# A hybrid decoder block on one core: taking POOL's work in the mixer to DVE, ACT and PE, and preparing the first stage's chunks one ahead

## The chip, the cores and the metric

One core of a Trainium2 chip runs the whole block. Its engines are PE (TensorE, matrix products), DVE (VectorE, elementwise work), ACT (ScalarE, activations and copies), POOL (GpSimd) and SP (SyncE, which here issues nearly all DMAs). The metric is device microseconds (us) of one execution, as a median of runs; less is better. PE's clock is granted at one of two levels, 2.4 GHz (shown as 1.0) and 1.2 GHz (0.5).

## The reference, cut to what matters

256 tokens of width 1024 in float32. `c` is one conditioning vector; `ada` holds 48 columns of 128 numbers.

```python
ada = (silu(c) @ w_ada + b_ada)                 # w_ada is 1024 x 6144
sh1, sc1, g1, sh2, sc2, g2 = split(ada, 6)
h = rmsnorm(x, norm_pre_mix) * (1 + sc1) + sh1
proj = h @ w_in + b_in                          # xr, gr, q, k, v, gate_r, gate_a
xr = causal_depthwise_conv(xr, conv_w, conv_b)
y_rnn = rg_lru(xr, ...) * gelu(gr)              # sigmoid gates, exp decay, scan over tokens
y_att = swa_sink_attention(q, k, v, sinks)      # 16 heads, window 128
merged = sigmoid(gate_r) * (y_rnn @ w_o_rnn) + sigmoid(gate_a) * (y_att @ w_o_attn)
x = x + g1 * rmsnorm(merged @ w_out, norm_post_mix)
h = rmsnorm(x, norm_pre_ffn) * (1 + sc2) + sh2
x = x + g2 * rmsnorm(moe_ffn(h, ...), norm_post_ffn)   # top 4 of 32 experts
```

The experts' weights come in 384 loads of 1024 KB; the whole kernel reads 466.61 MB.

## The kernel before, in words

All weights pass through one ring of 18 slots of 8 KB a partition (`ring`). SP issues the loads in program order, and a load waits until the slot that it takes is released, so a load's time follows the work that frees slots.

**First stage (0 to about 73 us).** The loop over `k` (L210 to L240) makes the first 2048 columns of the projection. Chunk `k` needs two groups of columns of `ada` and one block of rows of the weights. `ada_dot` (L130) makes 128 numbers of `ada` on DVE: it multiplies a 128x1024 tile of transposed `w_ada` by silu(c), and its accumulator gives the sums. Then `am` (scale and shift), `hT` (the modulated input), and `split` (L161), which makes of a weight tile the pair `hi` (rounded, on ACT, L167) and `lo` (the rest, L170) in two halves of 128x1024. The first half's `lo` is DVE's, the second's POOL's. PE then makes three products, hi*hi, hi*lo and lo*hi, 48 matmuls of 256 columns a chunk (chunk 0 alone is 16 plain float32 matmuls, L229).

**Middle stretch (about 73 to 268 us): the mixer.** 22 steps (`step`, L509), each 48 matmuls of 128x128 by 256 columns (L260; step 5 at L179) in a PSUM bank of tag "p", of which there are three, taken in turn. Step `i` first splits the weights of step `i+1`, then empties the bank of step `i-1` (`late_work`), then multiplies. `PLAN` gives, by hand, the small tasks that run in the middle of step `i` and after it: "A" is a late tile of `w_ada` (two `ada_dot`s; 16 such tiles), s and c the convolution, m and R the gates, g and h the gelu, d, D, q and S the decay and scan, M, X, E, N, T and P attention (scores, maximum, exponentials, normalising, transposes, product with v). Each engine works its queue in program order. POOL has `lo` of each second half and the products of R (L343), g (L351), h (L356) and N (`att_norm`, L452).

**After it.** w_out, the second norm and the router (to about 325 us); then 32 experts, for which SP streams 12 MB each.

Of the kernel before, what the change touches and what calls it, by code (L numbers as in the profile page):

```python
# [50 lines left out]
def tile_hybrid_block(ctx: ExitStack, tc: tile.TileContext, x_in, c, vecs, rows, w_ada, w_g1, w_qk, w_v, w_gate,  # L51
# [108 lines left out]

    def split(w, pool=True, mid=lambda: None):  # L161
# [47 lines left out]

    for k in range(KC):  # L210
        if k:
# [5 lines left out]
        wt = rtile((2048,), "w")  # L217
        for h in range(2):
            nc.sync.dma_start(out=wt[:, h * D:(h + 1) * D], in_=w_g1[k, :, h * D:(h + 1) * D])
        nc.vector.scalar_tensor_tensor(am[:, 0, k:k + 1], ada[:, 8 + k:9 + k], scb[:, k:k + 1], v("n_pre_mix", k),  # L220
                                       op0=OP.add, op1=OP.mult)
        nc.vector.tensor_tensor(am[:, 1, k:k + 1], ada[:, k:k + 1], vec[:, o_ + k:o_ + k + 1], op=OP.add)
        if k == 1:
            lru_scales()
        hT[k] = t2((S,), name="hT")
        nc.vector.tensor_scalar(hT[k], xnT[:, k], am[:, 0, k:k + 1], am[:, 1, k:k + 1], op0=OP.mult, op1=OP.add)
        if k < PLAIN:
            for f in range(16):
                nc.tensor.matmul(g1(f), wt[:, f * P:(f + 1) * P], hT[k], start=k == 0 and f % 2 == 0, stop=False,  # L229
                                 skip_group_check=True)  # L230
        else:
            whl = split(wt, mid=lambda: split_h(k))
            for h in range(2):
                for i, (m, n) in enumerate(THREE):
                    for f in range(8):
                        nc.tensor.matmul(g1(8 * h + f), whl[h][m][:, f * P:(f + 1) * P], (hTh, hTl)[n][:, k], start=False,
                                         stop=k == KC - 1 and i == 2, skip_group_check=True)
# [219 lines left out]
    def att_turn(pr, blk, kbs):  # L457
        for kb in kbs:
            for half in range(2):
                b = bank("a", (4, P))  # L460
                for g in range(4):
                    t = att_tile(pr, half, blk, 0 if blk == 0 else g // 2 * 2)
                    gi = g if blk == 0 else g % 2
                    nc.tensor.transpose(b[:, g], t[:, gi, kb * P:(kb + 1) * P], ident)
                pT = pTs[kb, half] = t2((4, P))
                if half == 0:
                    nc.scalar.activation(pT, b, AF.Copy)
                else:
                    nc.vector.tensor_copy(pT, b)

# [106 lines left out]
    for i in range(22):  # L577
# [768 lines left out]
```

## Time and profile before

| | us |
|---|---|
| Median of 3 runs (1271.99 to 1273.15) | 1272.44 |
| The profiled execution's own time | 1274.03 |
| Its span in the profile | 1272.4 |
| Busy: PE, DVE, ACT, POOL | 1156.7, 525.9, 261.5, 135.8 |

The profile is of one execution. Times of rows count from the start of its span. A busy engine is not an engine at its peak: what matters is which engine the others wait for in each stretch.

### The profile page before, as it was taken

The numbers are of one execution on the slowest core, as the hardware profiler recorded it, in microseconds if no ns is written. First come the engines' busy times: TensorE is split into PE (matmuls) and PEld (weight loads), VectorE is DVE, ScalarE is ACT, GpSimd is POOL, SyncE is SP. The second block draws the span as 40 slices with busy tenths as digits, with TensorE's granted clock in tenths as the row PEclk, the third lists the DMA queues.
The fourth block names the chain that finished last, engine by engine and source line by source line (L and its number), as shares of the span: only waits on it lengthen the run. The fifth ranks groups of instructions, "written<-read, shape, count | busy, mean of one in ns | idle before, by whom it ended". The sixth has DMA issues, their size and how long they took to land. (4 is left out here: it accounts for less than half of the span.)

```text
span 1272.4 us, 15323 instructions
## 1 busy us (share of the span) xinstructions
PE 1156.7 (91%) x5883; PEld 556.6 (44%) x5883; DVE 525.9 (41%) x914; ACT 261.5 (21%) x482; POOL 135.8 (11%) x79
## 2 busy tenths in 40 slices
PE   7897978869899999999999999999979999998886
PEld 5796757767433333333343333333323333332322
DVE  6999988965242222223221232322222323222222
ACT  4364656324311001010000011100100111000002
POOL 2455545321010000000000000000000000000000
PEclk9998989889999999999989989999979999999998
DMA  9963436667979999999999999999999999999995
GB/s 364 392 247 135 181 116 265 265 230 289 419 302 400 421 420 421 421 422 421 421 422 419 423 386 421 422 421 420 421 420 421 421 421 421 421 421 422 421 421 222
DMA packets 68176, 468.72 MB, mean 368 GB/s; under 512 B 7616, under 2 KB 8000, under 8 KB 13696
## 3 DMA queue, kind: packets, MB, share of 16 engines
q1 hardware_dynamic: 67392, 466.67, 89.6%
q10 hardware_dynamic: 704, 1.01, 0.3%
q8 instruction: 47, 0.77, 0.2%
q14 instruction: 33, 0.27, 0.1%
HBM read 466.61 MB, written 1.05 MB: 368 GB/s over the span
## 5 line engine op out<-in xcount | busy, mean ns | idle before, releaser
L964 PE MATMUL bank_a<-w,xg 128*64 128x512 f32 x2048 | 471.7, 606 | 11.2 <-DVEq L1126 6.5
L964 PEld LDWEIGHTS bank_a<-w,xg 128*64 128x64 f32 x2048 | 139.9, 139 | 292.8 <-issue 262.9
L997 PE MATMUL bank_a<-w,aT 128*64 128x512 f32 x960 | 216.8, 600 | 9.2 <-ACT aT L991 7.4
L1045 DVE TENSOR_SCALAR G<-bank_p,slot 128x256 fp32r<-128x256 f32 x32 | 15.5, 484 | 409.2 <-PE bank_p L1040 409.2
L997 PEld LDWEIGHTS bank_a<-w,aT 128*64 128x64 f32 x960 | 66.0, 137 | 142.1 <-issue 115.4
L991 ACT ACTIVATE aT<-bank_p 128x512 f32<-128x512 f32 x31 | 18.5, 597 | 524.7 <-PE bank_p L987 524.7
L1018 DVE TENSOR_TENSOR ff<-ff,bank_p 128x512 f32<-128x512 f32 x124 | 79.7, 684 | 64.7 <-PE bank_p L1015 64.7
L170 POOL TENSOR_TENSOR lo<-w,hi 128x1024 fp32r<-128x1024 f32 x32 | 89.2, 2789 | 132.5 <-ACT hi L167 105.7
L1260 POOL TENSOR_TENSOR os<-os,x 128x512 f32<-128x512 f32 x1 | 1.3, 1261 | 869.7 <-DVE rs L665 869.7
L131 DVE SCALAR_TENSOR_TENSOR w<-w,cs 128x1024 f32<-128x1024 f32 x48 | 89.0, 1892 | 1.0 <-DMA w<-in_w_ada_dram 1.0
L1005 DVE SCALAR_TENSOR_TENSOR ys<-bank_a,gslot,ys 128x512 fp32r<-128x512 f32 x31 | 23.3, 750 | 146.8 <-ACT ys L1004 146.8
L167 ACT ACTIVATE hi<-w 128x1024 fp32r<-128x1024 f32 x66 | 66.0, 1050 | 11.6 <-DVE lo L170 6.8
L1015 PE MATMUL bank_p<-ys,G 64*128 64x512 f32 x248 | 49.7, 474 | 14.3 <-DVE ys L1005 13.5
L1004 ACT ACTIVATE ys<-bank_a,gslot 128x512 fp32r<-128x512 f32 x31 | 21.3, 688 | 167.7 <-PE bank_a L997 164.1
L170 DVE TENSOR_TENSOR lo<-w,hi 128x1024 fp32r<-128x1024 f32 x34 | 46.8, 1381 | 6.5 <-ACT hi L167 6.5
L778 PE MATMUL bank_p<-pm,hth 128*128 128x256 f32 x112 | 31.9, 317 | 13.5 <-DVE pm L760 13.5
L1015 PEld LDWEIGHTS bank_p<-ys,G 64*128 64x128 f32 x248 | 20.4, 198 | 48.2 <-issue 25.2
L960 PE MATMUL bank_a<-b1r,pick 128*128 128x512 f32 x124 | 37.7, 423 | 0.0
L778 PEld LDWEIGHTS bank_p<-pm,hth 128*128 128x128 f32 x112 | 21.6, 192 | 35.9 <-issue 18.3
L977 ACT ACTIVATE ys<-gl 128x512 f32<-128x512 f32 x33 | 20.8, 630 | 74.9 <-DVE gl L976 74.9
L960 PEld LDWEIGHTS bank_a<-b1r,pick 128*128 128x128 f32 x124 | 20.7, 188 | 29.4 <-issue 26.8
L976 DVE TENSOR_SCALAR gl<-bank_a 128x512 f32<-128x512 f32 x33 | 22.6, 686 | 23.0 <-PE bank_a L964 17.2
(337 smaller groups left out, 1258.9 us busy)
## 6 DMA issues: line engine op xcount, KB each, us to landing
w<-in_w_dram SPq DMA_DIRECT2D x383, 1024.0 KB, 19.8
w<-in_w_ada_dram SPq DMA_DIRECT2D x16, 1024.0 KB, 5.0
w<-in_w_ada_dram SPq DMA_DIRECT2D x16, 512.0 KB, 10.1
w<-in_w_g_dram SPq DMA_DIRECT2D x16, 512.0 KB, 10.2
w<-in_w_gate_dram SPq DMA_DIRECT2D x8, 1024.0 KB, 5.8
w<-in_w_qk_dram SPq DMA_DIRECT2D x5, 1024.0 KB, 8.3
w<-in_w_oa_dram SPq DMA_DIRECT2D x4, 1024.0 KB, 6.8
w<-in_w_or_dram SPq DMA_DIRECT2D x4, 1024.0 KB, 5.9
```

Of the source, the lines that this page charges most:

```text
L131: nc.vector.scalar_tensor_tensor(wt[:, n], wt[:, n], 1.0, sc_, op0=OP.mult, op1=OP.mult, accum_out=ada[:, j:j + 1])
L167: nc.scalar.activation(hi[:, c_], w[:, c_], AF.Copy)
L170: (nc.gpsimd if h and pool else nc.vector).tensor_tensor(lo[:, c_], w[:, c_], hi[:, c_], op=OP.subtract)
L778: nc.tensor.matmul(ps[:, n], z[:, t, f * P:(f + 1) * P], pms[:, t].rearrange("p a b -> p (a b)"), start=t == 0 and n == 0 if len(ts) == 1 ...
L960: nc.tensor.matmul(o, m.rearrange("p a b -> p (a b)"), z, start=False, stop=False)
L964: nc.tensor.matmul(o[q * CAP:(q + 1) * CAP], xk(k), w1t[k][:, c0:c0 + 512], start=k == 0, stop=k == KC - 1)
L976: nc.vector.tensor_scalar(gl, bb[0], LIMIT, None, op0=OP.min)
L997: nc.tensor.matmul(y[q * CAP:(q + 1) * CAP], aT[:, k % 4, k // 4 * CAP:(k // 4 + 1) * CAP], w2t[k // 2][:, k % 2, q * 512:(q + 1) * 512], ...
L1004: nc.scalar.activation(hi, y, AF.Copy, scale=G[1])
L1005: nc.vector.scalar_tensor_tensor(lo, y, G[1], hi, op0=OP.mult, op1=OP.subtract)
L1015: nc.tensor.matmul(b[q], G[0][qs, t * P:(t + 1) * P], ys[i][qs], start=i == 1, stop=i == 0)
L1018: nc.vector.tensor_tensor(d, d, b[q], op=OP.add)
```

## The change

The order in `PLAN` and `ISSUE` stays. `split` gives both halves of `lo` to DVE. The products of R, h and N go from POOL to DVE; the gelu's polynomial becomes a Square on ACT and one product on DVE; the decay's square goes to ACT; the second half's copies of transposed probabilities (T) go from DVE to ACT; the emptying of `gr` goes to ACT and half of that of `xr` to DVE. Six of the 16 late tiles of `w_ada` (positions 2, 4, 5, 7, 9 and 11 of their order) come in untransposed layout, and PE multiplies them: `ada_mm` (8 matmuls with a stationary of 32 equal columns, four groups of output partitions, then a copy on ACT), and at the next list of tasks `ada_sum` (2 matmuls with one column, then a copy on ACT). In the first stage, iteration `k` prepares chunk `k` and then issues the matmuls of chunk `k-1`; `hT` is made on ACT, and silu(c) is made once more in another layout (`scc`).

```diff
+ON_PE = (2, 4, 5, 7, 9, 11)
...
     nc.scalar.activation(warm, eps, AF.Sqrt)
+    scc = consts.tile([P, KC], F32, name="scc")
+    nc.scalar.activation(scc, v("c"), AF.Sigmoid)
+    nc.vector.tensor_tensor(scc, v("c"), scc, op=OP.mult)
+    one_each = consts.tile([P, 1], F32, name="one_each")
+    nc.vector.tensor_reduce(one_each, ident.rearrange("p (a b) -> p a b", a=4)[:, :, 0], axis=AX.X, op=OP.add)
...
+    def ada_mm(wt):
+
+        b = bank("p")
+        for k in range(KC):
+            q = k % 4
+            nc.tensor.matmul(b[32 * q:32 * q + 32, 0:2 * P], scc[:, k:k + 1].to_broadcast([P, 32]),
+                             wt[:, k * 2 * P:(k + 1) * 2 * P], start=k < 4, stop=k >= 4)
+        r = wt[:, 0:2 * P]
+        nc.scalar.activation(r, b[:, 0:2 * P], AF.Copy)
+        return b, r
+
+    def ada_sum(b, r, j):
+
+        for n in range(2):
+            nc.tensor.matmul(b[:, 2 * P + n:2 * P + n + 1], r[:, n * P:(n + 1) * P], one_each, start=True, stop=True)
+        nc.scalar.activation(ada[:, j:j + 2], b[:, 2 * P:2 * P + 2], AF.Copy)
...
-            (nc.gpsimd if h and pool else nc.vector).tensor_tensor(lo[:, c_], w[:, c_], hi[:, c_], op=OP.subtract)
+            nc.vector.tensor_tensor(lo[:, c_], w[:, c_], hi[:, c_], op=OP.subtract)
...
+    for k in range(KC + 1):
+        if 0 < k < KC:
             wada.append(rtile((2, D), "w"))
...
+            def make_h(k=k):
+                nc.scalar.activation(hT[k], xnT[:, k], AF.Identity, scale=am[:, 0, k:k + 1], bias=am[:, 1, k:k + 1])
+                nc.scalar.activation(hTh[:, k], hT[k], AF.Copy)
+
+            if k < PLAIN:
+                make_h()
+                whl[k] = wt
+            else:
+                whl[k] = split(wt, make_h)
+                low_h(k)
+        if k:
+            m_ = k - 1
+            w_ = whl.pop(m_)
+            if m_ < PLAIN:
...
+                low_h(m_)
+            else:
+                for m, n in THREE:
+                    for f in range(16):
+                        nc.tensor.matmul(g1(f), w_[f // 8][m][:, f % 8 * P:(f % 8 + 1) * P], (hTh, hTl)[n][:, m_],
+                                         start=False, stop=m_ == KC - 1 and m == 1, skip_group_check=True)
...
     def ada_run(j):
+        if j in on_pe:
+            w = late[j].rearrange("p a b -> p (a b)")
+            sums_due.append((*ada_mm(w), 2 * j))
+            return
...
-        nc.gpsimd.tensor_tensor(i_, xcs[u], i_, op=OP.mult)
+        nc.vector.tensor_tensor(i_, xcs[u], i_, op=OP.mult)
...
-        nc.vector.tensor_tensor(z, g, g, op=OP.mult)
-        nc.vector.tensor_scalar(z, z, 0.044715, 1.0, op0=OP.mult, op1=OP.add)
-        nc.gpsimd.tensor_tensor(z, z, g, op=OP.mult)
+        nc.scalar.activation(z, g, AF.Square, scale=math.sqrt(0.044715))
+        nc.vector.scalar_tensor_tensor(z, z, 1.0, g, op0=OP.add, op1=OP.mult)
...
-        nc.gpsimd.tensor_tensor(g, z, g, op=OP.mult)
+        nc.vector.tensor_tensor(g, z, g, op=OP.mult)
...
-        nc.vector.tensor_tensor(z, a_, a_, op=OP.mult)
+        nc.scalar.activation(z, a_, AF.Square)
...
-            nc.gpsimd.tensor_tensor(t, t, den[:, blk, gs[0]:gs[0] + len(gs), None].to_broadcast(list(t.shape)),
+            nc.vector.tensor_tensor(t, t, den[:, blk, gs[0]:gs[0] + len(gs), None].to_broadcast(list(t.shape)),
...
-                if half == 0:
-                    nc.scalar.activation(pT, b, AF.Copy)
-                else:
-                    nc.vector.tensor_copy(pT, b)
+                nc.scalar.activation(pT, b, AF.Copy)
...
+        if f % 2:
+            nc.vector.tensor_scalar(xr[:, f, 3:], b_, v("b_xr", f), None, op0=OP.add)
+        else:
+            nc.scalar.activation(xr[:, f, 3:], b_, AF.Identity, bias=v("b_xr", f))
...
     def run(tasks):
 
+        while sums_due:
+            ada_sum(*sums_due.pop())
...
-                nc.vector.tensor_scalar(gr[:, f], b_, v("b_gr", f), None, op0=OP.add)
+                nc.scalar.activation(gr[:, f], b_, AF.Identity, bias=v("b_gr", f))
...
+    by_feature = a["w_ada"].T.reshape(48, P, D)[ada_order].reshape(24, 2, P, D).transpose(0, 2, 1, 3)
+    by_chunk = a["w_ada"].reshape(KC, P, 48, P)[:, :, ada_order].reshape(KC, P, 24, 2 * P).transpose(2, 1, 0, 3)
```

## Rows read from the trace of the kernel before

**Rows 1.** Windows: stretch, us, busy us (PE, PEld, DVE, ACT, POOL), clock, DMA share, GB/s
```profile
0.00:72.60 72.60, 58.58 (x396) 51.49 (x397) 59.73 (x101) 31.82 (x48) 24.42 (x19) 1.00 0.98 378
72.60:268.00 195.40, 169.29 (x1257) 151.81 (x1257) 182.10 (x241) 106.49 (x207) 97.49 (x47) 0.92 0.50 190
...
400.00:1015.00 615.00, 584.40 (x2690) 214.70 (x2687) 162.97 (x301) 59.66 (x108) 0.00 (x0) 0.98 1.01 419
1015.00:1236.00 221.00, 203.75 (x933) 69.97 (x931) 58.92 (x109) 20.50 (x36) 0.00 (x0) 1.00 1.01 421
```

**Rows 2.** Chain that ended last: start us, us, what
```profile
1015.70 19.77 DMA w<-in_w_dram
...
1235.39 1.94 PE bank_a L964 x8
```

**Rows 3.** Waits of PE, 72.6 to 268 us: total, times, longest (of seven lines)
```profile
PE bank_a L476 <- DVE t L469: 8.4, 2, 5.1
PE bank_a L406 <- DVE att L425: 6.2, 2, 4.8
```

**Rows 4.** Timeline of DVE, 60 to 156 us: start us, us, instruction
```profile
60.72 3.42 DVE L131 SCALAR_TENSOR_TENSOR w<-w,cs 128x1024 f32<-128x1024 f32 x1
...
64.07 1.21 DVE L131 SCALAR_TENSOR_TENSOR w<-w,cs 128x1024 f32<-128x1024 f32 x1
...
152.99 2.95 DVE L323 SCALAR_TENSOR_TENSOR xc<-xr,vec,xc 128x256 f32<-128x256 f32 x6
```

**Rows 5.** Timeline of POOL from 60 us
```profile
60.23 2.82 POOL L170 TENSOR_TENSOR lo<-w,hi 128x1024 fp32r<-128x1024 f32 x1 [4.49 <-ACT hi L167]
```

**Rows 6.** Groups by line on DVE, 72 to 268 us
```profile
L131 DVE SCALAR_TENSOR_TENSOR w<-w,cs 128x1024 f32<-128x1024 f32 x32 | 58.9, 1884 | 0.0
L170 DVE TENSOR_TENSOR lo<-w,hi 128x1024 fp32r<-128x1024 f32 x23 | 33.5, 1458 | 0.3 <-ACT hi L167 0.3
L323 DVE SCALAR_TENSOR_TENSOR xc<-xr,vec,xc 128x256 f32<-128x256 f32 x24 | 21.6, 918 | 0.6
...
L469 DVE COPY t<-bank_a 128x512 f32<-128x512 f32 x6 | 4.1, 683 | 1.8 <-POOL rnn L343 1.8
```

**Rows 7.** Waits of PE, 0 to 130 us
```profile
PE bank_p L236 <- ACT hTh L185: 8.8, 7, 1.6
```

**Rows 8.** Timeline of PE from 95 us
```profile
95.81 1.94 PE L334 MATMUL bank_a<-xc,cs 64*64 64x256 f32 x16
97.69 1.22 PE L260 MATMUL bank_p<-hTh,hi 128*128 128x256 f32 x8
98.75 1.12 PE L260 MATMUL bank_p<-hTl,hi 128*128 128x256 f32 x8
```

**Rows 9.** Timeline of ACT, first 34 us
```profile
7.20 1.28 ACT L121 ACT_TABLE_LOAD   x1
8.49 0.20 ACT L121 ACTIVATE small<-small 128x1 f32<-128x1 f32 x1
...
14.58 1.55 ACT L147 ACTIVATE xnT<-bank_a 128x512 f32<-128x512 f32 x3
```

**Rows 10.** Timeline of PE, first 30 us
```profile
14.59 2.86 PE L229 MATMUL bank_p<-hT,w 128*128 128x256 f32 x12 [0.86 <-DVE hT L226]
```

**Rows 11.** DMA issues of the page: KB each, median us to landing
```profile
w<-in_w_g_dram SPq DMA_DIRECT2D x16, 512.0 KB, 10.2
```

**Rows 12.** Groups by line on POOL, 72.6 to 268 us
```profile
L170 POOL TENSOR_TENSOR lo<-w,hi 128x1024 fp32r<-128x1024 f32 x23 | 64.6, 2810 | 64.7 <-ACT hi L167 53.4 <-DVE w L131 7.6 <-issue 2.2
L452 POOL TENSOR_TENSOR att<-att,den 128x512 f32<-128x512 f32 x12 | 13.9, 1184 | 11.4 <-DVE den L449 11.4
```

**Rows 13.** Timeline of PE, 236 to 345 us
```profile
273.78 1.87 PE L709 MATMUL bank_p<-rw,ada 128*128 128x32 f32 x16
...
285.64 1.12 PE L599 MATMUL bank_p<-ident,ada 128*128 128x128 f32 x4 [9.52 <-DVE t L569]
```

**Rows 14.** Groups by line on ACT, 72 to 270 us
```profile
L443 ACT ACTIVATE att<-att,nm 128x128 f32<-128x128 f32 (+1 forms) x32 | 14.1, 444 | 0.0
```

More of the change, by code (lines that the diff above doesn't have):

```diff
@@ L41 @@
                ("b_xr", 8), ("b_gr", 8), ("b_q", 8), ("b_k", 2), ("b_ga_r", 8), ("b_ga_a", 8),
-               ("cw0", 8), ("cw1", 8), ("cw2", 8), ("cw3", 8), ("cb", 8), ("rba", 8), ("rbx", 8), ("lam", 8)):
+               ("cw0", 8), ("cw1", 8), ("cw2", 8), ("cw3", 8), ("cb", 8), ("rba", 8), ("rbx", 8), ("lam", 8), ("c", 8)):
     VEC[_n] = (_o, _w)
@@ L158, in tile_hybrid_block, with split @@
     nc.vector.memset(xr[:, :, 0:3], 0.0)
-    def split(w, pool=True, mid=lambda: None):
+    def split(w, mid=lambda: None):
         hi, lo = [ring.tile([P, 2 * D], F32R, name=n_, tag="w") for n_ in ("hi", "lo")]
@@ L182, in tile_hybrid_block @@
     hTl = ring.tile([P, KC, S], F32R, name="hTl", tag="w")
-    def split_h(k):
-        nc.scalar.activation(hTh[:, k], hT[k], AF.Copy)
-        nc.vector.tensor_tensor(hTl[:, k], hT[k], hTh[:, k], op=OP.subtract)
     def lru_scales():
@@ L208, in g1, with low_h @@
         return g1b[f // 2][:, (f % 2) * S:(f % 2 + 1) * S]
-    for k in range(KC):
-        if k:
+    def low_h(k):
+        nc.vector.tensor_tensor(hTl[:, k], hT[k], hTh[:, k], op=OP.subtract)
+    whl = {}
+    for k in range(KC + 1):
+        if 0 < k < KC:
             wada.append(rtile((2, D), "w"))
@@ L216, in tile_hybrid_block @@
             ada_dot(wada[k], 1, 8 + k)
[L217 to L230, printed above, removed]
-        else:
-            whl = split(wt, mid=lambda: split_h(k))
-            for h in range(2):
[L234 to L237, printed above, removed]
@@ L238, in tile_hybrid_block @@
-        if 4 <= k < 4 + PLAIN:
-            split_h(k - 4)
+        if k < KC:
+            wt = rtile((2048,), "w")
+            for h in range(2):
+                nc.sync.dma_start(out=wt[:, h * D:(h + 1) * D], in_=w_g1[k, :, h * D:(h + 1) * D])
+            nc.vector.scalar_tensor_tensor(am[:, 0, k:k + 1], ada[:, 8 + k:9 + k], scb[:, k:k + 1], v("n_pre_mix", k),
+                                           op0=OP.add, op1=OP.mult)
+            nc.vector.tensor_tensor(am[:, 1, k:k + 1], ada[:, k:k + 1], vec[:, o_ + k:o_ + k + 1], op=OP.add)
+            if k == 1:
+                lru_scales()
+            hT[k] = t2((S,), name="hT")
+            def make_h(k=k):
[7 more added lines that the diff above has]
+                low_h(k)
@@ new lines, in tile_hybrid_block @@
+        if k:
[3 more added lines that the diff above has]
+                for f in range(16):
+                    nc.tensor.matmul(g1(f), w_[:, f * P:(f + 1) * P], hT[m_], start=m_ == 0 and f % 2 == 0, stop=False,
+                                     skip_group_check=True)
+                low_h(m_)
+            else:
+                for m, n in THREE:
+                    for f in range(16):
+                        nc.tensor.matmul(g1(f), w_[f // 8][m][:, f % 8 * P:(f % 8 + 1) * P], (hTh, hTl)[n][:, m_],
+                                         start=False, stop=m_ == KC - 1 and m == 1, skip_group_check=True)
@@ L297, in tile_hybrid_block @@
     late = {}
+    sums_due = []
     def ada_run(j):
+        if j in on_pe:
+            w = late[j].rearrange("p a b -> p (a b)")
+            sums_due.append((*ada_mm(w), 2 * j))
+            return
         for n in range(2):
@@ L465, in att_turn @@
                 pT = pTs[kb, half] = t2((4, P))
-                if half == 0:
-                    nc.scalar.activation(pT, b, AF.Copy)
-                else:
-                    nc.vector.tensor_copy(pT, b)
+                nc.scalar.activation(pT, b, AF.Copy)
     def att_apply(pr, blk):
@@ L489, in tile_hybrid_block @@
     order = [(E // 2 + i) % E for i in range(E)]
-    w_in_, whl, w1_first = {}, {}, []
+    w_in_, w1_first = {}, []
     rest = [*range(8, 12), *range(16, 20), *range(12, 16), *range(20, 24)]
     order_a = list(rest)
+    on_pe = [rest[i] for i in ON_PE]
     assert "".join(ISSUE.values()).count("w") == NW and "".join(ISSUE.values()).count("a") == len(rest)
@@ L512, in step @@
         if i + 1 < NW:
-            whl[i + 1] = split(w_in_[i + 1], i < 24)
+            whl[i + 1] = split(w_in_[i + 1])
         for f in late_work:
@@ L534, in tile_hybrid_block @@
         b_ = g1b[f // 2][:, (f % 2) * S:(f % 2 + 1) * S]
-        nc.scalar.activation(xr[:, f, 3:], b_, AF.Identity, bias=v("b_xr", f))
+        if f % 2:
+            nc.vector.tensor_scalar(xr[:, f, 3:], b_, v("b_xr", f), None, op0=OP.add)
+        else:
+            nc.scalar.activation(xr[:, f, 3:], b_, AF.Identity, bias=v("b_xr", f))
     bks = {}
     def run(tasks):
+        while sums_due:
+            ada_sum(*sums_due.pop())
         for task in tasks.split():
@@ L584, in tile_hybrid_block @@
                 b_ = g1b[4 + f // 2][:, (f % 2) * S:(f % 2 + 1) * S]
-                nc.vector.tensor_scalar(gr[:, f], b_, v("b_gr", f), None, op0=OP.add)
+                nc.scalar.activation(gr[:, f], b_, AF.Identity, bias=v("b_gr", f))
         run(after)
+    assert not sums_due
     nc.vector.tensor_tensor(ada[:, 16:48], ada[:, 16:48], vec[:, o_ + 16:o_ + 48], op=OP.add)
@@ L1308 @@
     ada_order = [j for k in range(8) for j in (k, 8 + k)] + list(range(16, 48))
-    w_ada = a["w_ada"].T.reshape(48, P, D)[ada_order].reshape(24, 2, P, D).transpose(0, 2, 1, 3)
+    by_feature = a["w_ada"].T.reshape(48, P, D)[ada_order].reshape(24, 2, P, D).transpose(0, 2, 1, 3)
+    by_chunk = a["w_ada"].reshape(KC, P, 48, P)[:, :, ada_order].reshape(KC, P, 24, 2 * P).transpose(2, 1, 0, 3)
+    late = [*range(8, 12), *range(16, 20), *range(12, 16), *range(20, 24)]
+    w_ada = by_feature.copy()
+    for i in ON_PE:
+        w_ada[late[i]] = by_chunk[late[i]].reshape(P, 2, D)
     vecs = np.concatenate([cols(z) for z in (
@@ L1312 @@
         bi[0], bi[1], bi[2], bi[3], bi[5], bi[6], a["conv_w"][0], a["conv_w"][1], a["conv_w"][2], a["conv_w"][3],
-        a["conv_b"], a["rg_b_a"], a["rg_b_x"], a["rg_lambda"])], axis=1)
+        a["conv_b"], a["rg_b_a"], a["rg_b_x"], a["rg_lambda"], a["c"])], axis=1)
     rows = np.concatenate([bi[4], a["attn_sinks"], a["router_b"]])[None]
```

## The prediction, made before the change was run

> **What bounds the kernel now.** I read the windows first, cut where the program's stages meet [rows 1]. From 400 us on the DMA engines are full (share 1.01, 419 to 421 GB/s) in both stretches, and the chain that ended last runs over the experts' loads from 1015.70 to 1235.39 us, with only PE's short end behind [rows 2]. So the end is the start of that full stream plus a fixed number of bytes: a microsecond taken from the mixer, where the DMA share is 0.50, moves the end by a microsecond, since the loads follow the slots that the mixer frees. A microsecond on any engine after 400 us is worth nothing. In the middle stretch (195.4 us) DVE is busy 182.1 us, PE 169.3 at a granted clock of 0.92, ACT 106.5, POOL 97.5. DVE is the engine without air; PE's idle 26 us there are nearly all waits for DVE, led by 8.4 us for copies of attention (L469) and 6.2 for its maxima (L425) [rows 3].
>
> Why DVE is so full is seen in two neighbouring rows: of two equal `ada_dot`s, the one that meets POOL's `lo` (60.23 us, 2.82 long) takes 3.42 us and ends about when POOL ends, the next one, alone, 1.21 [rows 4, 5]. In the middle stretch the mean is 1.884 for the dots, 1.458 for `lo`, 0.918 for the convolution's 256 columns [rows 6]. So much of DVE's 182 us is waiting on POOL, inside its instructions.
>
> **First stage.** PE waits 8.8 us in all for the chunks after the first [rows 7]; the period is set by DVE: the long dot 3.42, the clear one 1.21, and a chain of small steps through ACT. Afterwards DVE has two dots, two `lo` of the second kind (4 times 1.21, 4.9) and, by my estimate, 0.6 of small ones, 5.5 us a chunk, against PE's 48 matmuls at 0.12 (eight in 0.96, from 98.75 minus 97.69 with the start-up of 0.1 left out), 5.8 [rows 8]. PE is then the bound and, with a chunk ready ahead, waits no more: minus 8.8 us. Against it stands the start. The new Sigmoid for `scc` comes behind the warm Sqrt, and the Sqrt of the norm behind it needs its table again: two loads of 1.28 [rows 9] and 0.2, so 2.7 us later. And `hT` of chunk 0 is now made by ACT, behind the four copies that end at 16.1 in the row, where DVE had it for the first matmul at 14.59 [rows 9, 10]: 16.1 plus 0.4 (under the 0.52 of one of those three copies, which have twice the columns) plus 2.7 is 19.2, so PE starts 4.6 us later. PE's idle time before it grows too; half clock for part of chunk 0 I put at 0.9 (between 0 and 2). Net minus 3.3 (between minus 1 and minus 6).
>
> The loads cover this. SP's order is unchanged, and of the 18 slots three are held throughout, so at four slots a chunk the weights of chunk 7 wait until PE has used `hi` of chunk 3. By the times above that is near 42 us; with 10.2 us to landing [rows 11] they are there at 52, and DVE, 5.5 a chunk after a start near 25, comes to them at 53. Each us that they are later is a us lost.
>
> The row shows the load at 1.28 us with the activation 0.01 behind it. The Trainium skill (ScalarE: Activation LUTs, What ACT_TABLE_LOAD costs) gives 2.66 us a switch with the drain, which would make the start 2.8 us worse; the trace does not show that drain.
>
> **Middle stretch, DVE.** With POOL silent I price by the clear row, 1.21 to 1.22:
> - dots: 32 become 20, 58.9 to 24.4
> - `lo`: 23 become 46, 33.5 to 56.1
> - convolution: 24 at 0.49 (six together, clear of POOL, took 2.95 [rows 4]) instead of 0.918, 21.6 to 11.8
> - from POOL: 12 products of N and 12 of R, g and h, all 128x512, at 0.68 (the size of L469 [rows 6]; POOL took 1.184 [rows 12]): plus 16.3
> - gone to ACT or merged: six copies, eight emptyings of 256 columns, the squares and scalings, some 22 passes of that size: minus 14
> - the rest, 182.1 less those three groups, 68.1, holds contention too: I estimate that 9 of it go, between 0 and that.
>
> Sum 24.4 + 56.1 + 11.8 + 16.3 - 14 + 68.1 - 9 = 154 us (163 if the rest keeps its contention), down from 182.
>
> **Middle stretch, PE.** The 22 steps are 1056 matmuls at 0.12, 127 us; 22 times 5.76. The small products (L334 in 1.9 a time [rows 8], scores, transposes, v) add some 28, counted at full clock: 155. That agrees with 169.3 busy less what the half clock costs (0.08 of 195.4, at most 15.6).
>
> New on PE: `ada_mm`, eight float32 matmuls of 256 columns. No row shows four groups side by side. Lower end: the pairs of L964 run two groups of 512 columns in 0.97 (eight records, 1.94, are two pairs [rows 2]), so four groups of 256 might take 0.5 and eight matmuls 1.0. Upper end: one after another as in L229 (12 records, 2.86, are six matmuls, 0.45 each [rows 10]): 3.6. I take 1.0, since L964 too splits output partitions into groups. `ada_sum` is two small ones at 0.23 (16 records of L709 in 1.87 are eight [rows 13]), 0.5. Six tiles: 9 us (up to 25).
>
> Changing the tile shape costs something: behind L334 (64*64) the first eight matmuls take 1.22 where the next take 1.12, so 0.1 [rows 8]; 12 switches, 1.2 us, lie inside my rounding. The Trainium skill (TensorEngine Tiling (Array Packing), Key Properties) says that changing the tiling mode drains the engine; the 0.1 is what the trace shows of that.
>
> So PE's floor is 155 + 9 = 164, DVE 154 to 163, ACT about 120 (106.5 and some 14 for the passes moved to it). PE becomes the bound, with little air on DVE.
>
> **What is still waited for.** The order in `PLAN` is unchanged, and ACT now stands where DVE stood. After step 5 come two tiles on PE and E; there are three banks "p", and step 6 takes the one that step 5 filled, so PE waits until DVE has emptied it. DVE's queue there holds D, whose square waits on ACT behind E's eight exponentials (14.1 / 4 = 3.5 us and about 1.5 of accumulator reads [rows 14]), then two `lo`, 2.4. From the last scores to there PE has v's 5.8, two tiles at 1.0 and the next scores (1.2), 9 us; the other two have the maxima (3), E (5), the square and its product (1.2), `lo` (2.4) and the emptying (0.7), one behind the other, 12 to 13: about 4 us. The waits for copies of transposed probabilities move from DVE to ACT, which has E's 5 us in front in steps 7 to 10: three places at some 2, so 6 of the 8.4. Steps 13 to 16 (three scans) and 19 (two tiles): 3. Half clock behind such gaps: 3. Together 16 (between 5 and 25). Stretch: 164 + 16 = 180 against 195.4, minus 15.4.
>
> The slots of the six tiles come free at `ada_sum`, half a step after PE has read them; no weight of the mixer was waited for by ACT's `hi` in this stretch, and the DMA share of 0.50 leaves room, so I price that at nothing (its cover gone, a step's split would wait for one landing).
>
> **Tail to 325 us.** `lo` moves to DVE in front of merge_r (plus 1.2), whose products lose POOL's contention (my estimate: minus 1.6). The 9.5 us that PE waits there [rows 13] hang on the b1 loads that ACT waits for; they stay. Minus 0.4.
>
> Sum: 3.3 + 15.4 + 0.4 = 19.1 off 1274.03 is 1254.9; the median of before lies 1.6 under its profiled execution, so 1253.3, say 1253.
>
> **Rivals.**
> - *PE floor.* ACT keeps up and the waits shrink under 9 us, the start costs less. For it: ACT has 75 us of air in the stretch. Against it: three engines at 120 to 164 of 175 in fixed order. Gain 26 to 35: 1238 to 1246.
> - *ACT or DVE takes over.* The queues stand behind one another in the order given, and waits come to 25 or more, or `ada_mm` runs one after another (6 times 2.6, plus 15.6). Gain 4 to 13: 1260 to 1269.
> - *The end doesn't move.* If the expert loads started when they do now, by bandwidth alone, the time would stay 1272. Against it: share 0.50 in the mixer, and loads that wait for slots.
> - *Slower: DVE's long rows are its own.* If a dot stays 1.884 and `lo` 1.458 with POOL idle, DVE's stretch gets 182.1 - 22.6 + 33.5 + 16.3 - 14 = 195.3, and with the 13 us that it idled 208: plus 13; first-stage chunks get plus 0.9 each (another `lo`, less `hT`), with 4.6 at the start plus 11. 1296. The point is a mean of about 1.37 per 128x1024 pass: 66 of them, 92 of others and 13 idle make 195. The two neighbouring rows speak against it.
>
> **How the numbers follow.** Forecast 0.62, 1246 to 1260; floor 0.12; ACT, DVE or `ada_mm` 0.16; end unmoved 0.04; slower 0.06. The predicted time is the first's, 1253. The range 1240 to 1264 takes in most of the floor and half of the third case, whose bounds (waits 5 to 25, `ada_mm` 1.0 to 3.6, start 1 to 6) are those above. Within 0.2% (2.5 us) a measurement of this kernel can't tell from no change: faster 0.90, same 0.04, slower 0.06.
>
> **What would show it.** Dots and `lo` at 1.22 throughout; the first matmul near 19 us, chunks every 5.8 to 5.9, and the first stage ending near 69; PE with the longest busy time in a middle stretch of some 180; one `ada_mm` within 1 us; a wait near 4 us ahead of step 6; the expert stream full some 19 us earlier, and the same 421 GB/s after it. I am wrong if a new table load or copy on ACT stands ahead of PE in most steps, if DVE rows stay long, or if the stream's start does not move.

## The result, and the profile after

The changed kernel takes 1257.2 us (median of 4 runs, 1255.7 to 1258.1) against 1272.8 for the kernel before on the same chip (4 runs, 1272.0 to 1273.2): ratio 0.9877, 95% interval 0.986 to 0.9895. It is faster by 1.2%. The profiled execution took 1256.5 us with a span of 1254.9, 17.5 less than before.

In the code of the changed kernel the lines have moved: `ada_dot` is L137, `hi` and `lo` L190 and L193, the first stage's products L267 and L273, a step's products L295, the emptying of v's bank L319, `ada_mm` and its copy L145 and L148, `ada_sum` and its copy L154 and L155, `merge_r` L612 and L613 (it adds the recurrent half's output projection to `merged`, and its first product empties a PSUM bank), the broadcast behind it L643, the rounding of b1 L664 (b1 is the bias of the experts' first layer), the experts' first products L1008.

The windows of the changed kernel, cut where its stages meet (the first products, the first step, the end of w_in's and the output projections' steps, the first expert; the columns are those of [rows 1]):

```profile
0.00:19.50 19.50, 10.64 (x27) 6.04 (x27) 9.85 (x27) 13.25 (x20) 2.50 (x12) 0.84 0.89 338
19.50:69.00 49.50, 49.50 (x370) 48.07 (x371) 40.42 (x81) 24.32 (x36) 0.00 (x0) 0.96 1.01 398
69.00:248.00 179.00, 166.89 (x1378) 150.02 (x1377) 143.97 (x235) 118.79 (x241) 0.47 (x4) 0.97 0.55 214
248.00:306.40 58.40, 45.52 (x222) 35.64 (x220) 28.91 (x75) 20.30 (x41) 0.00 (x0) 0.88 0.77 289
400.00:1000.00 600.00, 569.64 (x2616) 210.44 (x2614) 159.18 (x293) 58.11 (x105) 0.00 (x0) 0.98 1.01 419
1000.00:1218.00 218.00, 200.78 (x919) 68.98 (x917) 56.75 (x105) 19.86 (x35) 0.00 (x0) 1.00 1.01 421
```

Read against [rows 1]: the first stage ends at 69.0 instead of 72.6, the middle stretch takes 179.0 instead of 195.4, and what follows up to the first expert 58.4, where the kernel before took 56.4 (this window of before, 268.00 to 324.40 us, has PE busy 45.26). So 3.6 and 16.4 are won and 2.0 lost; the first expert starts 18.0 us earlier, and the span is 17.5 shorter. The experts' stream is as full as before, at 419 to 421 GB/s. In the middle stretch PE is idle for 12 us, DVE for 35.

The groups of DVE in that stretch, to be read against [rows 6]:

```profile
L193 DVE TENSOR_TENSOR lo<-w,hi 128x1024 fp32r<-128x1024 f32 x44 | 51.8, 1220 | 14.3 <-ACT hi L190 14.3
L137 DVE SCALAR_TENSOR_TENSOR w<-w,cs 128x1024 f32<-128x1024 f32 x20 | 23.6, 1219 | 0.0
L364 DVE SCALAR_TENSOR_TENSOR xc<-xr,vec,xc 128x256 f32<-128x256 f32 x24 | 11.2, 483 | 0.6
L465 DVE SCALAR_TENSOR_TENSOR att<-nd,bank_a 128x128 f32<-128x128 f32 (+1 forms) x32 | 9.4, 347 | 0.5 <-PE bank_a L446 0.5
L467 DVE TENSOR_REDUCE mx<-att 128x2 f32<-128x512 f32 (+1 forms) x12 | 8.2, 686 | 0.4
L492 DVE TENSOR_TENSOR att<-att,den 128x512 f32<-128x512 f32 x12 | 7.6, 687 | 0.1
```

Every long row has the length of the clear row of before: 1.22 for a dot and a `lo`, 0.483 for a column of the convolution, 0.687 for a product that POOL took 1.184 for [rows 12].

The largest waits of PE up to 400 us (total, times, longest):

```profile
PE bank_p L643 <- DVE t L612: 11.2, 1, 11.2
PE bank_p L295 <- DVE vv L319: 9.3, 1, 9.3
PE bank_a L169 <- ACT xn L161: 5.5, 1, 5.5
```

The first is the tail's, 9.52 before [rows 13]. The second, 9.3 us in one piece, stands ahead of step 6; all others of the middle stretch come to 2.8 us. The waits for the first stage's chunks (8.8 before, [rows 7]) are gone. How the 9.3 us come about is seen in the timelines of ACT, of DVE and of PE around them:

```profile
92.24 0.38 ACT L148 ACTIVATE w<-bank_p 128x256 f32<-128x256 f32 x1 [2.88 <-PE bank_p L145]
98.58 0.17 ACT L155 ACTIVATE ada<-bank_p 128x2 f32<-128x2 f32 x1 [5.96 <-PE bank_p L154]
98.65 0.62 ACT L395 ACTIVATE rnn<-rnn 128x512 f32<-128x512 f32 x1
...
116.76 0.39 ACT L483 ACTIVATE att<-att,nm 128x128 f32<-128x128 f32 x1
...
120.26 0.61 ACT L408 ACTIVATE t<-rnn 128x512 f32<-128x512 f32 x1
```

```profile
99.31 0.69 DVE L396 TENSOR_TENSOR gr<-rnn,gr 128x512 f32<-128x512 f32 x1 [2.74 <-ACT rnn L395]
...
113.13 0.75 DVE L465 SCALAR_TENSOR_TENSOR att<-nd,bank_a 128x256 f32<-128x256 f32 x2
...
120.91 0.69 DVE L409 SCALAR_TENSOR_TENSOR rnn<-t,rnn 128x512 f32<-128x512 f32 x1 [4.30 <-ACT t L408]
122.38 2.36 DVE L193 TENSOR_TENSOR lo<-w,hi 128x1024 fp32r<-128x1024 f32 x2 [0.79 <-ACT hi L190]
124.66 0.69 DVE L319 TENSOR_TENSOR vv<-bank_p,row 128x512 f32<-128x512 f32 x1
```

```profile
105.58 1.14 PE L446 MATMUL bank_a<-kT,qT 64*128 64x256 f32 x8
```

ACT reaches the copy of an `ada_sum` at 92.6 and stands there for 5.96 us, since PE makes that sum only later; the sigmoid behind it (L395), which waits for nothing of PE, starts at 98.65, and DVE idles 2.74 us for it. From then on DVE works almost without a gap, and it comes late: PE has made the last scores ahead of E at 106.72, but DVE reaches their maxima only at 113.13, 6.4 us later. Then E's exponentials occupy ACT from 116.76, the square of D behind them starts at 120.26, DVE waits 4.30 us for it, and two `lo` come before DVE empties v's bank at 124.66. Step 6 starts at 125.40.

### The profile page after: what moved, and what is told of

Its sections match the earlier page's. It is cut to its first block, busy times and chain, and to the rows that moved or that the text cites. A ratio compares the mean times of both kernels' runs of the same rounds, so it can differ in the third digit from the quotient of the medians.

```text
span 1254.9 us, 15487 instructions
## 1 busy us (share of the span) xinstructions
PE 1156.5 (92%) x6003; PEld 558.9 (45%) x6003; DVE 479.5 (38%) x918; ACT 279.5 (22%) x523; POOL 10.4 (1%) x23
## 5 line engine op out<-in xcount | busy, mean ns | idle before, releaser
L1008 PE MATMUL bank_a<-w,xg 128*64 128x512 f32 x2048 | 471.3, 605 | 11.4 <-PEq L1170 6.6
L1008 PEld LDWEIGHTS bank_a<-w,xg 128*64 128x64 f32 x2048 | 139.9, 139 | 293.6 <-issue 261.6
L193 DVE TENSOR_TENSOR lo<-w,hi 128x1024 fp32r<-128x1024 f32 x66 | 78.3, 1220 | 26.9 <-ACT hi L190 26.9
L190 ACT ACTIVATE hi<-w 128x1024 fp32r<-128x1024 f32 x66 | 66.1, 1052 | 6.1 <-DVE lo L193 4.2
L137 DVE SCALAR_TENSOR_TENSOR w<-w,cs 128x1024 f32<-128x1024 f32 x36 | 42.5, 1220 | 0.0
L295 PE MATMUL bank_p<-hTh,hi 128*128 128x256 f32 x208 | 31.5, 295 | 9.3 <-DVE vv L319 9.3
L295 PEld LDWEIGHTS bank_p<-hTh,hi 128*128 128x128 f32 x208 | 27.3, 195 | 13.2 <-DVE vv L319 9.8
```

Source lines behind the costliest of these rows:

```text
L193: nc.vector.tensor_tensor(lo[:, c_], w[:, c_], hi[:, c_], op=OP.subtract)
L295: nc.tensor.matmul(b[:, n], w[n][m][:, k * P:(k + 1) * P], z[l][:, k], start=k == 0 and i == 0 and (n == 0 or not late), stop=k == KC - 1 ...
L1008: nc.tensor.matmul(o[q * CAP:(q + 1) * CAP], xk(k), w1t[k][:, c0:c0 + 512], start=k == 0, stop=k == KC - 1)
```

## The experiments

All runs of the experiments stand beside runs of the kernel before on the same chip; what is compared is the ratio to it. 0.001 is 1.27 us; "us against the changed kernel" is the difference of the ratios times that, and as each ratio is known to some 0.0015, such a difference is known to about 3 us. The start of the first expert's products, from each profile, is given beside it (306.4 in the changed kernel). In the seven traces whose start is the changed kernel's own, the first product comes between 19.3 and 20.3 us; so a difference of the first expert of under 1 us says nothing.

| | median us | ratio (95%) | us against the changed kernel | first expert |
|---|---|---|---|---|
| e11 before, all `lo` on DVE | 1251.68 | 0.9832 (0.9818 to 0.9847) | -5.7 | 300.7 |
| e5 half of `lo` back on POOL | 1266.49 | 0.9929 (0.9909 to 0.9948) | +6.6 | 315.8 |
| e6 not one ahead | 1258.24 | 0.9878 (0.9858 to 0.9897) | +0.1 | 308.0 |
| e1 start | 1253.07 | 0.9836 (0.9823 to 0.985) | -5.2 | 302.6 |
| e2 fifth tile on DVE | 1252.83 | 0.9831 (0.9818 to 0.9845) | -5.9 | 302.0 |
| e3 no tile on PE | 1251.06 | 0.9823 (0.981 to 0.9837) | -6.9 | 300.3 |
| e12 e1 and e3 | 1249.36 | 0.98 (0.9786 to 0.9813) | -9.8 | 300.2 |
| e7 order at step 6 | 1249.41 | 0.9801 (0.9786 to 0.9816) | -9.7 | 300.0 |
| e4 b1 later | 1245.74 | 0.9777 (0.9763 to 0.979) | -12.7 | 294.7 |
| e8 e1, e3, e4 | 1236.87 | 0.9703 (0.9687 to 0.9719) | -22.2 | 287.5 |
| e9 e1, e4, e7 | 1236.33 | 0.9707 (0.9691 to 0.9722) | -21.6 | 286.7 |
| e10 e1, e3, e4, e7 | 1232.41 | 0.9673 (0.9659 to 0.9688) | -26.0 | 284.9 |

**Where the gain comes from: `lo` alone (e11).** One line of the kernel before:

```diff
-            (nc.gpsimd if h and pool else nc.vector).tensor_tensor(lo[:, c_], ...)
+            nc.vector.tensor_tensor(lo[:, c_], ...)
```

> The kernel before with one edit: DVE makes both halves of every `lo`; N, R, the sums and copies stay where they were. Theory (POOL's passes are paid a second time in DVE's rows): DVE gets 32 passes of 1.21 us more and gives back more than that in shorter dots (mean 1.884 down to 1.4 or less), `lo` and convolution rows; the first stage loses its waits; 5 to 18 us under the kernel before. Rival (DVE only exchanges long rows for more rows, the gain of the change came from the work that ACT and PE took): within 3 us of the kernel before.

It is 21 us faster than the kernel before (1273.23 to 1251.68), more than the theory's range, and faster than the whole change. The first expert starts 23.7 us earlier: the first stage gives 6.7 of it, the middle stretch 18.1, and the tail takes 1.1 back. Its window of the middle stretch, and its groups of DVE from 68 to 262 us:

```profile
65.90:243.20 177.30, 162.94 (x1258) 148.09 (x1258) 169.88 (x259) 106.37 (x207) 36.98 (x29) 0.97 0.57 220
```

```profile
L170 DVE TENSOR_TENSOR lo<-w,hi 128x1024 fp32r<-128x1024 f32 x45 | 58.6, 1341 | 0.3 <-ACT hi L167 0.3
L131 DVE SCALAR_TENSOR_TENSOR w<-w,cs 128x1024 f32<-128x1024 f32 x32 | 40.9, 1320 | 0.0
L323 DVE SCALAR_TENSOR_TENSOR xc<-xr,vec,xc 128x256 f32<-128x256 f32 x24 | 14.3, 612 | 0.6
L425 DVE SCALAR_TENSOR_TENSOR att<-nd,bank_a 128x128 f32<-128x128 f32 (+1 forms) x32 | 9.3, 342 | 0.0
L427 DVE TENSOR_REDUCE mx<-att 128x2 f32<-128x512 f32 (+1 forms) x12 | 8.2, 686 | 0.4
```

The first three groups are 113.8 us; in [rows 6] the same three are 114.0, with 22 `lo` fewer. DVE does 22 passes more in the same time: what POOL had done in 64.6 us [rows 12] DVE had paid for in full, inside its own rows. Over the stretch DVE is busy 169.9 us instead of 182.1, so its other rows became shorter too. That POOL's `lo` simply came late for PE is not the cause in this stretch: of its waits there before, only 0.2 us are for POOL. The last two groups, which have one operand in PSUM or one operand in all, are as long as in the changed kernel, where POOL is silent (347 and 686 ns).

**The reverse (e5):** in the changed kernel, `(nc.gpsimd if h else nc.vector)` for `lo`.

> The changed kernel with the second 1024 columns of every `lo` on POOL again, as in the kernel before; all else stays. Theory (POOL's work lengthens DVE's rows): DVE gives away some 33 passes of 1.21 us, but its dots and remaining `lo` that meet POOL's 2.8 us passes come out between 1.21 and 3.4 again, the mean of a dot over 1.6, and the time is 5 to 15 us over the changed kernel. Rival (DVE's rows do not depend on POOL, the gain came from the other edits): the dots stay at 1.22, DVE is relieved by some 40 us, and the time is the same or up to 5 us less.

Plus 6.6 us by the ratios and plus 11.0 by the spans (the profiled execution of e5 is the slowest of its four). Its groups of DVE from 69 to 260 us:

```profile
L193 DVE TENSOR_TENSOR lo<-w,hi 128x1024 fp32r<-128x1024 f32 x22 | 37.7, 1715 | 11.8 <-ACT hi L190 11.8
L137 DVE SCALAR_TENSOR_TENSOR w<-w,cs 128x1024 f32<-128x1024 f32 x20 | 27.4, 1409 | 0.0
L364 DVE SCALAR_TENSOR_TENSOR xc<-xr,vec,xc 128x256 f32<-128x256 f32 x24 | 17.5, 745 | 0.6
```

DVE has 22 `lo` fewer than the changed kernel and is busy 82.6 us with the three groups, where that has 86.6: POOL's work relieves DVE of 4 us, and each `lo` that it makes is there 2.67 us after its start instead of 1.22. The mean of a dot, 1.41, stayed under the 1.6 expected; the time came out as the theory said.

**One ahead (e6):** the matmuls of chunk `k` stand in pass `k` again.

```diff
-    for k in range(KC + 1):
-        if 0 < k < KC:
+    for k in range(KC):
+        if k:
...
-        if k < KC:
+        if True:
...
-        if k:
-            m_ = k - 1
+        if True:
+            m_ = k
```

> The changed kernel with the first stage's one-ahead order undone: the matmuls of chunk k are issued right behind the preparation of chunk k, as before. Theory (the matmuls stand on PE's queue alone, so their place in the program text moves nothing on the other engines; what ended PE's waits for chunks is DVE without POOL's contention): no more than 1.5 us either way, PE's waits for chunks stay under 1 us. Rival (being one ahead was what removed them): the 8.8 us of waits of the kernel before come back, the time is 5 to 9 us more.

Ratio 0.9878, no difference. PE waits 1.5 us for chunks, six times 0.23 to 0.30, instead of nothing, a little over the 1 us that was expected; the first expert starts 1.6 us later, 0.8 of it because the first product came later. The 8.8 us of [rows 7] do not come back.

**The start (e1).**

```diff
-    nc.scalar.activation(warm, eps, AF.Sqrt)
     (the Sigmoid of scc)
+    nc.scalar.activation(warm, eps, AF.Sqrt)
```

> The changed kernel with the Sigmoid for scc moved ahead of the warm Sqrt, so that ACT loads its tables twice less at the start. Theory (the start is a chain on ACT): the two loads of 1.28 us go, the first float32 matmul comes near 16.9 us in place of 19.5, part of the half clock around it goes, and since PE sets the first stage's pace all of it reaches the end: 3 to 5 us less, 1252 to 1254. Rival (the first stage is fed by the DMA engines at share 1.0, whatever the start): PE waits for chunks later and the end moves by under 1 us.

Timeline of ACT, first of the changed kernel, then of e1:

```profile
6.59 1.28 ACT L122 ACT_TABLE_LOAD   x1
7.88 0.20 ACT L122 ACTIVATE small<-small 128x1 f32<-128x1 f32 x1
8.10 1.28 ACT L124 ACT_TABLE_LOAD   x1
9.39 0.21 ACT L124 ACTIVATE scc<-vec 128x8 f32<-128x8 f32 x1
...
11.10 1.28 ACT L158 ACT_TABLE_LOAD   x1 [0.45 <-DVE junk L132]
```

```profile
6.89 0.19 ACT L123 ACTIVATE scc<-vec 128x8 f32<-128x8 f32 x1
7.10 1.28 ACT L125 ACT_TABLE_LOAD   x1
8.39 0.20 ACT L125 ACTIVATE small<-small 128x1 f32<-128x1 f32 x1
```

Two table loads are gone, and the first product starts at 16.46 instead of 19.49, 3.0 us earlier. The Trainium skill (ScalarE: Activation LUTs, What ACT_TABLE_LOAD costs) has 2.66 us a switch, 5.3 for two; the start moved by 3.0, which is the two rows of 1.28 and 0.5 around them. Over all traces the first product comes at 16.2 to 17.1 with the Sigmoid ahead (five) and at 19.3 to 20.3 without (seven). The first stage ends 3.0 us earlier too (66.0), the first expert starts 3.7 earlier; the 5.2 by the ratios agree within their error.

**The tiles on PE (e2, e3).** `ON_PE = (2, 4, 5, 7, 9, 11)` becomes `(2, 4, 7, 9, 11)` in e2 and `()` in e3.

> The changed kernel with five tiles on PE: the second of the two tiles after step 5 goes back to DVE. Theory (the wait of 9.3 us ahead of step 6 comes from the bank: with two extra banks taken, step 6 needs the one that step 5 filled): the wait falls under 2 us, the half clock behind it goes, 8 to 11 us less, 1246 to 1249. Rival (DVE and ACT are simply late there, behind the exponentials): the same wait returns one or two steps later and the time falls by 0 to 4 us.

> The changed kernel with all 16 late tiles on DVE, none on PE. Theory (PE is the bound of the middle stretch, so its extra 9.5 us of matmuls and the waits that came with them cost more than the 14.6 us of DVE that they save): DVE at about 158 busy in a middle stretch of some 165 to 173, 6 to 13 us less. Rival (without PE's help DVE is the bound again): waits for lo and for maxima return on PE and the time is 2 to 10 us more.

Both gain. In e2 the wait of 9.3 us is gone and two others of together 5.1 stand in its place, in part the rival's; the time falls by 5.9 us, between the two ranges. In e3, PE's two largest waits up to 400 us:

```profile
PE bank_a L446 <- DVE att L465: 10.6, 1, 10.6
PE bank_p L643 <- DVE t L612: 9.8, 1, 9.8
```

ACT's waits for `ada_sum` and `ada_mm` are gone. In the middle stretch, 176.3 us long instead of 179.0, PE is busy 160.1 us instead of 166.9, DVE 158.5 instead of 144.0. So the tiles on PE take 6.8 us of PE's time and spare DVE time that it had. The gain is within the theory's range, but the stretch did not shrink to the 165 to 173 us expected, and the rival's wait for maxima is there too. It is 6.9 us by the ratios and 6.0 by the first expert; 2.7 of these lie in the stretch and 3.2 in the tail (55.2 us instead of 58.4, with a shorter wait for b1). In e12 the stretch is as short (176.5 us); the tail's part is 3.4 in e8 beside e4, but under 1 in e12 beside e1 and in e10 beside e9, and why is not shown. A long wait at step 6 is there in the changed kernel and in e3; in e3 it is the scores that wait for DVE.

**What is left of the change without its two losses (e12: e1 and e3 together).**

> The changed kernel without its two parts that cost time alone: the Sigmoid of `scc` ahead of the warm Sqrt (5 us alone) and the six tiles back on DVE (6.9 alone); b1 and the order around step 6 as in the changed kernel. What is compared is the kernel before with `lo` alone moved to DVE, at a ratio of 0.9832. Theory (the rest of the change, N and R to DVE, sums and copies to ACT, merged emptyings, still gives a few us beyond `lo`): ratio 0.977 to 0.981, 3 to 8 us under it. Rival (`lo` was all of it, the rest is worth nothing): ratio 0.982 to 0.985.

Ratio 0.98 against e11's 0.9832, which would be 4 us for the rest of the change (N, R, sums, copies). But e12's profile has a span of 1250.3 against e11's 1249.1 (e12's profiled execution is the slowest of its five, e11's the fastest), its first expert starts 0.5 us earlier, and its middle stretch is 0.7 us shorter. Whether the rest is worth anything stays open between nothing and some 4 us.

**The order at step 6 (e7).**

```diff
-5: ('d0 M02', 'X02 E00 D0 A M10 A')
+5: ('d0 M02', 'D0 X02 E00 A M10 A')
...
         issue(3 * i)
+        if i == 6:
+            for f in late_work:
+                f()
+            late_work.clear()
         if i + 1 < NW:
             whl[i + 1] = split(w_in_[i + 1])
```

> The changed kernel with two moves around step 6: D0 (ACT's square, DVE's product) is issued ahead of E00's exponentials, and DVE empties the bank of v ahead of the split for step 7 instead of behind it. Theory (PE's wait of 9.3 us there is the sum of a square queued on ACT behind the exponentials and two `lo` queued on DVE ahead of the emptying): it shrinks to 5 or less, some of it returns as a wait at the next use of the split, and the time falls by 4 to 9 us. Rival (all engines are equally late there, the wait only moves on): the 9.3 us are found again within the next two steps, and the time changes by less than 2 us.

Timeline of DVE there:

```profile
113.31 0.68 DVE L409 SCALAR_TENSOR_TENSOR rnn<-t,rnn 128x512 f32<-128x512 f32 x1
...
117.30 0.68 DVE L319 TENSOR_TENSOR vv<-bank_p,row 128x512 f32<-128x512 f32 x1
122.65 2.36 DVE L193 TENSOR_TENSOR lo<-w,hi 128x1024 fp32r<-128x1024 f32 x2 [4.67 <-ACT hi L190]
```

The product of D waits for nothing, the emptying comes at 117.30 instead of 124.66, and PE waits 1.8 us instead of 9.3. Step 6's first 24 products take 3.14 us instead of 4.86, since they no longer run at half clock. Of these 9.2 us 3.5 return: 2.2 in waits of under 1 us behind it, the rest as busy time of PE. The middle stretch takes 173.3 us instead of 179.0, at a granted clock of 1.00, and the first expert starts 6.3 us earlier. The two moves were not run apart, so what each of them gives is not shown.

**b1 later (e4).** The copies of b1 to its float32r parts, on ACT and DVE, stand behind the steps of w_out (float32r is the rounded type that `hi` and `lo` have too); the loads stay where they were.

```diff
-    for h in range(2):
-        nc.scalar.activation(b1r[:, h], b1t[h], AF.Copy)
-        nc.vector.tensor_tensor(b1r[64:, h], b1t[h][64:], b1r[64:, h], op=OP.subtract)
... (the steps of w_out)
+    (the same three lines)
```

> The changed kernel with the rounding and subtraction of b1 (ACT and DVE) issued after the four steps of w_out in place of ahead of them; the loads stay where they are. Theory (in the tail PE waits 11.2 us because ACT and DVE stand at the b1 loads with hi, lo and merge_r behind them): the wait falls to 2 to 5 us and 7 to 10 us go from the time. Rival (the wait is for the expert and w_out loads, or for merge_r's own chain): the time moves by under 2 us.

In the changed kernel, ACT's timeline shows what the copies did to its queue:

```profile
256.52 0.63 ACT L664 ACTIVATE b1r<-t 128x512 fp32r<-128x512 f32 x1 [5.83 <-DMA t<-in_b_dram]
262.35 0.63 ACT L664 ACTIVATE b1r<-t 128x512 fp32r<-128x512 f32 x1 [5.20 <-DMA t<-in_b_dram]
262.89 1.99 ACT L190 ACTIVATE hi<-w 128x1024 fp32r<-128x1024 f32 x2
```

11 us of two waits for small loads, with the `hi` of w_out behind them and DVE's `lo` and merge_r behind that. In e4 PE's wait there is 1.9 us instead of 11.2, and the time falls by more than the 7 to 10 us expected: 12.7 by the ratios, 11.7 by the first expert.

**Together (e8, e9, e10).** e8 is e1, e3 and e4; e9 is e1, e4 and e7, with the tiles on PE; e10 is all four.

> Three edits that each gained alone, together: the Sigmoid of `scc` ahead of the warm Sqrt (5 us alone by the ratios, 4.2 by the spans), the six tiles back on DVE (6.9 alone), b1's copies moved behind the steps of w_out (12.7 alone). Theory (they lie at three different places of the same serial path ahead of the expert stream): the gains add up, 20 to 25 us under the changed kernel, 1233 to 1238. Rival (a later wait absorbs part of it): under 17 us, over 1241.

> The changed kernel with the Sigmoid of `scc` ahead of the warm Sqrt, b1's copies behind the steps of w_out, and D0 and the emptying of v's bank moved forward; the six tiles stay on PE. Theory (three places of one serial path: 5, 12.7 and 7.5 us alone): 21 to 26 us under the changed kernel, 1232 to 1237. Rival (the wait ahead of step 6 comes back once the rest is earlier, because it hangs on loads): under 18 us.

> The same with the six tiles on DVE as well. Theory (on PE they cost 6 x 1.57 us of PE and block ACT's queue at `ada_sum`; the 10.6 us that PE waits ahead of step 6 without them are D's square behind E, which the new order takes away): 3 to 6 us under the same kernel with the tiles on PE, and 27 to 32 under the changed kernel. Rival (what the tiles cost alone, 6.9 us, was nearly all the wait ahead of step 6, which is now gone either way, and DVE has no room for 15 us more): the two versions differ by less than 2 us, or the one with the tiles on PE is the faster.

Most of the gains add up: 22.2 us where the single ones give 24.8, 21.6 where they give 27.6. All four together give 26.0 of 34.5, since e3 and e7 both work on step 6; that is one less than the 27 to 32 expected. e10 is the fastest kernel: 1232.4 us, 3.3% under the kernel before. It lies 4.3 us under e9 by the ratios, as the theory had it; but its first expert starts 1.8 us earlier and its span is 1.0 shorter, so the difference may be as small as the rival's. Its middle stretch takes 171.4 us against 173.3, with PE busy 159.6 against 166.4: most of what the tiles no longer take of PE is a wait again, for the scores at step 6:

```profile
PE bank_a L446 <- DVE att L465: 6.2, 1, 6.2
```

In e9, where PE makes the six tiles, no wait of the stretch is over 1.8 us.

## Why the prediction was right, and where its steps were not

- **What bounds the kernel: right.** The first expert's products start 18.0 us earlier and the span is 17.5 shorter; in the changed kernel and all twelve experiments the span ends between 947.4 and 950.3 us after that start.
- **DVE's rows: right, their sum 10 us too high.** All of them came out at the clear price (1.22, 0.483, 0.687), and e11 and e5 show that POOL is the cause, in both directions. One reading was off: the long dot of [rows 4] ends not when POOL's `lo` ends (63.05 us) but 1.09 us later, at 64.14, nearly its own 1.22; it waits for POOL's row and then runs. DVE was busy 144.0 us where 154 to 163 were forecast: two `lo` fewer fell into the stretch (2.4), neighbouring rows overlap by 0.08 us each, which the sum had not taken off (some 3), and the other rows took 4.0 less. So "little air on DVE" was wrong; it had 35 us. The rule that fits is in the Trainium skill (SBUF — State Buffer, Who interferes with whom): a DVE instruction with two SBUF inputs contends with a GpSimd instruction that reads SBUF, one with a single SBUF input in its plain mode does not. The trace agrees: dots, `lo` and the convolution change with POOL's work, the scores' rows (343 ns before, 347 after) and the maxima (686 in both) do not. In the kernel before, 24 of the 32 scores' rows run beside a row of POOL, as here, where the dot ahead of them is stretched to 3.36 (POOL, then DVE; the last line is the same scores in the changed kernel):

```profile
109.07 6.62 POOL L170 TENSOR_TENSOR lo<-w,hi 128x1024 fp32r<-128x1024 f32 x2
...
110.12 3.36 DVE L131 SCALAR_TENSOR_TENSOR w<-w,cs 128x1024 f32<-128x1024 f32 x1
...
113.41 0.87 DVE L425 SCALAR_TENSOR_TENSOR att<-nd,bank_a 128x128 f32<-128x128 f32 x4
...
102.81 0.88 DVE L465 SCALAR_TENSOR_TENSOR att<-nd,bank_a 128x128 f32<-128x128 f32 x4
```

- **First stage: the sum right, its reason not.** The first product came at 19.49 (19.2 forecast), the stage ended at 69.0 (69). But "with a chunk ready ahead, waits no more" is not what ended the waits: with the order undone (e6) they are 1.5 us, and with `lo` alone moved (e11) 2.3 of 8.8. POOL's contention was the cause; the order ahead is worth 1.6 us at most. The start's two loads cost 3.0 as shown by e1 (2.7 forecast). Chunk 0 lost 2.0 us to the clock (its 16 products take 9.2 us, 7.2 before) where 0.9 was put. That the sum came out all the same is luck: a chunk after the first keeps PE busy for 5.8 us instead of 6.0, 1.4 us in all that the forecast did not have.
- **PE's floor: right.** 166.9 busy against 164 (166.5 in e7, at a granted clock of 1.00); the sixteen records of one `ada_mm` take 1.07 us (1.0), `ada_sum` 0.5.
- **What is still waited for: the term mis-sized in both parts.** Forecast were 4 us ahead of step 6, 9 of other waits and 3 of clock. There were 9.3, 2.8, and the half clock behind the 9.3. The place was right, with E, D's square and two `lo` one behind the other, as e7 shows by taking them apart; missing were the 6.4 us by which DVE was already late when it came there. ACT works its queue in order, and the copies behind `ada_mm` and `ada_sum` waited in it for 5.8 and 15.1 us in the stretch; for 5.96 us of these the timeline above shows ready work behind them, and 7.3 come only with PE's own long wait. The sum (179.0 against 180) came right by luck: 5.3 too little ahead of step 6 and 6.2 too much elsewhere nearly cancel.
- **The six tiles: not weighed.** The prediction priced them on PE (9 us) and took them for part of the relief. With POOL silent DVE had the room itself, and on PE they cost 6.9 us net by the ratios (e3), of which 2.7 are seen in the stretch, and still 1 to 4 when the waits around them are mended (e9 against e10).
- **Tail: wrong in sign.** Minus 0.4 was forecast, plus 2.0 measured, 1.7 of it in PE's wait (11.2 against 9.52). Behind the second copy of b1 DVE has two `lo` (2.32 us) where one of them was POOL's before: 1.1, as priced. The copies of b1 end 0.6 later, counted from where PE stops. The contention did go, 1.4 us of it, but at the wrong place: `merge_r`'s second product shrank (below, before and after), and PE waits for the first, ahead of it. And the wait that "stays" need not: it is an order in ACT's queue, worth 12.7 us (e4).

```profile
285.62 2.13 DVE L570 TENSOR_TENSOR mg<-mg,t 128x512 f32<-128x512 f32 x1
...
266.95 0.69 DVE L613 TENSOR_TENSOR mg<-mg,t 128x512 f32<-128x512 f32 x1
```

- **The median.** Forecast for the profiled execution were 1254.9 us, measured 1256.5. The median of before lay 1.6 under its profiled execution, that of the change lies 0.7 over its own; this is more than half of the 4.2 us between 1253 and 1257.2.

The change is thus one edit that gains 21 us and others that together give back 5.7, by the ratios and by the first expert alike. The start and the six tiles are where it is lost: without both (e12) the kernel is as fast as e11 or up to 4 us faster.

## What to carry to other kernels

Where one engine's rows stretch another's, work taken off the first can be free on the second: compare a row that meets the other engine with one that doesn't, and count the passes that would fit in. When an edit bundles one cause with much else, run the cause alone; here a single line beat the whole. A copy whose producer comes late in PE's queue, or whose load has only just been issued, does not belong in an in-order queue ahead of work that is ready; the second of these was tried by itself here (e4), the first only seen in the trace.

## What the hardware showed that was not expected

- POOL's passes were no help at all: with 22 of them moved over, DVE's three groups took 113.8 us instead of 114.0.
- DVE's row waits for the whole of POOL's: in the first 300 us of the kernel before, 23 dots and `lo` start inside a row of POOL, and 22 of them end 1.08 us behind that row's end, however long they had waited (the other one starts 0.06 ahead of the end). Those that start ahead of POOL's row keep their 1.2 us. So a pass of POOL that DVE meets costs DVE up to 2.2 us (3.42 less 1.22), more than the 1.22 of making it.
- One long wait of PE was followed by half clock: the granted clock is 0.51 from 119.0 to 129.3 us, within and behind the 9.3 us ahead of step 6, and the first 24 products there take 4.86 us. Without that wait (e7) they take 3.14, and the whole stretch runs at 1.00.

```profile
119.00:129.30 10.30, 3.90 (x18) 3.90 (x19) 7.51 (x16) 4.30 (x11) 0.00 (x0) 0.51 0.00 0
```
